# Expert stage of a two-block network: the token gather cut in quarters and spread over the expert pairs, slot gates as one-pass products, expert choice beside group choice

## The chip, the cores and the metric

One core of one Trainium2 chip runs the whole program. The metric is device microseconds (us) of one execution, as the median of several. Durations below come from one profiled execution of the kernel before. Engines: PE is TensorE, DVE is VectorE, ACT is ScalarE, POOL is GpSimd; SP issues most of the transfers.

## The reference, cut to what matters

The program is two blocks over 256 tokens of width 1024. The first block mixes four branches and ends in a wide feed-forward. The second has two layers, each an attention followed by a mixture of experts. The change touches only the mixture of experts, which runs twice:

```python
def moe_ffn(x, router_w, router_b, w_gate, w_up, w_down):      # 256 tokens, 16 experts in 4 groups
    scores = sigmoid(xt @ router_w)
    biased = (scores + router_b).reshape(T, 4, 4)
    group_score = top_k(biased, 2)[0].sum(-1)                   # two best of each group
    best_group = argmax(group_score)
    local = top_k(biased[best_group], 2)[1]                     # two best experts of the best group
    gate = scores[chosen] / sum
    ...                                                         # tokens sorted by expert
    yb = (silu(xi @ w_gate[e]) * (xi @ w_up[e])) @ w_down[e]    # per expert: 1024 -> 256 -> 1024
    y = sum of yb * gate over the token's two experts
```

In front of it stands `layer_norm(ALPHA * x + mixed)`, and another one follows it.

## The kernel before, in words

Activations lie with features on the partitions, as eight blocks of 128 features by 256 tokens. The Tile framework writes out each engine's queue when the program is built. It goes by program order and by its own estimates of what is ready. `behind(ins)` adds an order: what is traced in it is queued after `ins` on that engine. The second block's expert stage (`moe`, L1596) goes like this.

**Routing** (`into_experts` L1404, `route` L1490). Logits come from a small product. On DVE follow sigmoid and bias, then the sum of each group's two best, then `among_first` (L1478), which counts for each entry how many of its four stand before it: once on the group scores (the result is `gb`, the best group) and once on the 16 experts (`sel`). Small products turn `sel` into running counts. `at` is each token's place in an expert's 64 slots, and `places` (L1537) compares it with 1 to 64. The result is `oneh`, one one-hot column for each of 16 x 64 slots. DVE makes `oneh` in four operations of 512 columns (8 experts and 128 tokens each). In between, PE runs products of ones that nobody reads (`warm`, L250): 24 while the routing is computed (`WARM["stats"]`) and 3 before the gather (`WARM["places"]`). The tokens themselves are normalised, transposed and cut in a high and a low part (`tok`, in the trace `s<-half`), four pieces of 256 features. The low parts are DVE's, the first queued behind the group choice, the others behind the last `places`.

**Gather** (L1615). `xg` holds the 1024 slots' tokens, made as one-hot products: a quarter is 256 slots (four experts, two pairs), eight feature blocks, and four one-pass products for each block (two token halves, high and low part). Each feature block has a PSUM bank of the tag `acc` to itself, and ACT and DVE take the blocks in turns to SBUF (`taken`).

**Slot gates** (L1636). 18 products of `oneh` (as plain float32) with the 16 columns of token gates bring each slot's gate to the slot's partition (`gslot`). They run in one batch.

**Expert pairs.** For each pair, `into` (L1664) multiplies the pair's slots with the gate and up weights into the one bank `ps` (32 PE instructions). `hidden` applies silu and the slot gate and transposes through the one bank `tr`. `down` (L1699) multiplies with the down weights into two banks `y`. `across` (L1654) transposes the one-hots, two pairs at a time, into the one tile `oht`. `back` (L1719) adds the pair's result to the four accumulators `acc`. `down` and `back` run one and two pairs late. A ninth pass, the spare one (i = 8), serves one expert with more than 64 tokens. Its weights are fetched by POOL's indirect transfers, since the expert is known only at run time. It stands third in the order (`SPARE = 2`). `late_norm` (L520) normalises the residual in six parts, which are spread over the passes (`LATE`).

**Order of the gather before.** Quarter 0 comes ahead of the first pair's `into`. Quarters 1 and 2, the spare slots' plan and all slot gates come behind it. Quarter 3, the spare slots' gather and two of five `across` come behind the second pair's `into`. The accumulators are allocated only then, since the gather uses their banks.

**Weights** come as pieces of 512 KB: eight for a pair's `into`, four for its `down`, six for the spare pass, 102 in a layer. They land in 21 buffers in turns (13 `raw`, 4 `whi`, 4 `wlo`), so a piece waits until the one 21 before it has been read. SP issues all but the spare ones, in one fixed order.

Of the kernel before, what the change touches and what calls it, by code (L numbers as in the profile page):

```python
# [8 lines left out]
F32 = mybir.dt.float32  # L9
F32R = mybir.dt.float32r  # L10
# [6 lines left out]
D = 1024  # L17
# [184 lines left out]
class Kern:  # L202
# [1275 lines left out]
    def among_first(self, out, val, n, cmp, count):  # L1478

        other = val[:, :, None, :].to_broadcast([128, n, 4, 4])  # L1480
        own = val[:, :, :, None].to_broadcast([128, n, 4, 4])
        self.tt(cmp[:, :, :, 0:4], other, own, OP.is_gt)
        self.tt(cmp[:, :, :, 4:8], other, own, OP.is_equal)
        tri = self.k["tri4"].rearrange("p (a b) -> p a b", a=4)
        self.tt(cmp[:, :, :, 4:8], cmp[:, :, :, 4:8], tri[:, None].to_broadcast([128, n, 4, 4]), OP.mult)
        red = self.A.tile([128, n, 4], F32, name=f"r_red{n}")
        self.nc.vector.tensor_reduce(red, cmp, axis=AX.X, op=OP.add)
        return self.ts(out, red, float(count), OP.is_lt)

    def route(self, sc):  # L1490


        nc, A, X = self.nc, self.A, self.X

        def T(name, *shape):
            return A.tile([128] + list(shape), F32, name=name)
        self.sc, self.bi = sc, X.tile([128, 2, 16], F32, name="r_bi")
        self.ts(sc, sc, 1.0, OP.add)
        nc.vector.reciprocal(sc, sc)
        self.tt(self.bi, sc, self.rb[:, None, :].to_broadcast([128, 2, 16]), OP.add)  # L1500
# [3 lines left out]
        gsf, gtf = (i.rearrange("p t g -> p (t g)") for i in (gs, gt))  # L1504
        self.tt(big, v[:, :, 0:4:2], v[:, :, 1:4:2], OP.max)
# [7 lines left out]
        f4 = lambda t: t.rearrange("p t (g e) -> p (t g) e", g=4)  # L1513
        self.sel = sel = X.tile([128, 2, 16], BF, name="r_sel")
# [71 lines left out]
    def gates(self):  # L1586
# [7 lines left out]
        return sc  # L1594

    def moe(self, layer, x):  # L1596

# [14 lines left out]
            else:  # L1612
                self.ts(out, src, g, OP.mult, o, OP.add)

        def gather(h):  # L1615
            c = slice(h * 256, h * 256 + 256)
            for k in range(8):
                p = self.ps("acc")[:, :256]
                f = slice(k * 128, k * 128 + 128)
                for t in range(2):  # L1620
                    for i in range(2):
                        self.mm(p, xt[i][:, t, f], oh[:, t, c], t == 0 and i == 0, t == 1 and i == 1)
                taken(k, xg[:, k, c], p)

        def gather_spare():
            p = self.ps("acc")
            for k in range(8):
                f = slice(k * 128, k * 128 + 128)
                for t in range(2):
                    for i in range(2):  # L1630
                        self.mm(p[:, k * SLOTS:k * SLOTS + SLOTS], xt[i][:, t, f], ohs[:, t, 0],
                                k == 0 and t == 0 and i == 0, t == 1 and i == 1)
            for k in range(8):
                taken(k, xs_[:, k], p[:, k * SLOTS:k * SLOTS + SLOTS])

        def slot_gates(gates, over):  # L1636

            p = self.ps("tr")
            for i in range(9):
                for t in range(2):  # L1640
                    l = ohf[:, t, i * 128:i * 128 + 128] if i < 8 else ohs[:, t].rearrange("p a s -> p (a s)").bitcast(F32)
                    self.mm(p[:, i * 16:i * 16 + 16], l, gates[:, t], i == 0 and t == 0, t == 1)
            gs = A.tile([128, 9], F32, name="gslot")
            for s in range(2):
                r = slice(64 * s, 64 * s + 64)
                nc.vector.tensor_copy(gs[r, 0:8], p[r, s:s + 8 * 18:18])
            t16 = A.tile([128, 16], F32, name="sp_t2")
            nc.vector.tensor_tensor_reduce(t16, p[:, 128:144], over, 1.0, 0.0, OP.mult, OP.add, accum_out=gs[:, 8:9])
            return gs

        yparts = self.big([128, 2, 2, D])
        yparts = [yparts[:, i] for i in range(2)]

        def across(i):  # L1654

            n = min(2, 9 - i)
            p = self.ps("tr")
            for c in range(2 * n):
                j, t = i + c // 2, c % 2
                o = ohf[:, t, j * 128:j * 128 + 128] if j < 8 else ohs[:, t].rearrange("p a s -> p (a s)").bitcast(F32)  # L1660
                nc.tensor.transpose(p[:, c * 128:c * 128 + 128], o, ident)  # L1661
            self.act(oht[:, i:i + n], p[:, :n * S].rearrange("p (g t) -> p g t", g=n), AF.Copy)

        def into(i):  # L1664

# [53 lines left out]
        def back(i, y, j0, j1, first, last):  # L1719
            for j in range(j0, j1):  # L1720
                f = slice(j * 128, j * 128 + 128)
                for k in range(2):
                    self.mm(acc[j // 2][:, j % 2 * S:j % 2 * S + S], y[:, k, f], oht[:, i],
                            first and k == 0 and j % 2 == 0, last and k == 1)
# [10 lines left out]
        for n, i in enumerate(order):  # L1735
            p = into(i)
            if n == 0:
                gather(1)
                gather(2)
                over, ohs, rows = self.spare(layer)  # L1740
                gs = slot_gates(gates, over)
            elif n == 1:
                wsp = self.spare_weights(rows)
                gather(3)
                gather_spare()
                oht = self.big([128, 9, S])
                across(0)
                across(2)
                acc = [self.ps("acc") for _ in range(4)]
            elif n == 2:  # L1750
                for c in (4, 6, 8):
                    across(c)
            if n in LATE:
                next(norm)
            with self.behind(*self.last_mm):
                if n > 1:
                    back(*ys.pop(0), 0, 8, n == 2, False)
                if prev is not None:
                    ys.append((prev[0], down(*prev)))
            with self.behind(*self.last_mm):  # L1760
                prev = i, hidden(i, p)
        self.raws, self.turn = raws, -1
        back(*ys.pop(0), 0, 8, False, False)
        y = down(*prev)
        self.ln_begin()
# [132 lines left out]
```

## Time and profile before

| | us |
|---|---|
| median of 3 runs | 1334.96 (1331.76 to 1335.94) |
| profiled execution | 1333.13 |
| its span, first to last instruction | 1331.3 |
| PE busy | 1291.8 (97%) |
| DVE busy | 737.2 (55%) |
| ACT busy | 622.5 (47%) |

The expert stage of layer 0 takes roughly 844 to 1012 us of the span and that of layer 1 roughly 1152 to 1313 us. PE's busy share is high all along, but PE matmuls are pipelined and a product at half the clock also counts as busy. So the stage is read by what each batch of products took, by the granted clock of each stretch, and by the chain of work that ended last.

### The profile page before, as it was taken

How to read it: one execution, taken by the hardware profiler on the slowest of the kernel's cores; microseconds unless marked ns; L12 is line 12 of the kernel's file. 1: busy time of each engine (PE TensorE's matmuls, PEld its weight loads, DVE VectorE, ACT ScalarE, POOL GpSimd, SP SyncE). 2: the span in 40 equal slices, each digit the busy share in tenths (PEclk: the TensorE clock that was granted, in tenths of full speed). 3: DMA queues.
4: the chain of work that ended last, by engine and by line, in shares of the span. 5: the costliest groups of instructions: out<-in, count | busy, mean ns of one | idle time of the engine just before them, and what ended most of it. 6: DMA issues, size and time to landing. Idle time of an engine off the chain costs nothing.

```text
span 1331.3 us, 23153 instructions
## 1 busy us (share of the span) xinstructions
PE 1291.8 (97%) x9421; PEld 1073.0 (81%) x9421; DVE 737.2 (55%) x1378; ACT 622.5 (47%) x965; POOL 20.8 (2%) x41
## 2 busy tenths in 40 slices
PE   9999999999999999999999999999998999999996
PEld 7887899999999999999999999573445999664443
DVE  7887665657555556875556463523117676533115
ACT  5756864445544446645454544333115665324112
POOL 0000000000000000000000000010000000010000
PEclk9999999999999999999999999989998999999998
DMA  7441456566486555665555554488995542358992
GB/s 255 129 165 38 133 185 210 180 190 213 160 297 203 184 179 177 187 193 156 169 166 164 163 163 132 163 326 294 407 409 187 158 127 80 127 156 297 380 399 67
DMA packets 90307, 265.16 MB, mean 199 GB/s; under 512 B 26432, under 2 KB 26576, under 8 KB 89936
## 3 DMA queue, kind: packets, MB, share of 16 engines
q1 hardware_dynamic: 86720, 253.07, 57.0%
q0 software_dynamic: 3472, 10.53, 2.3%
q8 instruction: 76, 1.25, 0.4%
q14 instruction: 39, 0.32, 0.1%
HBM read 264.53 MB, written 6.89 MB: 204 GB/s over the span
## 4 chain that ended last, share of the span: by engine, by line
PE 69%; DVE 3%; DMA 2%; ACT 1%; issue 1%; SPq 0%; DVEq 0%; ACTq 0%
PE ps L248 40%; PE acc L248 16%; PE y L248 5%; PE sc L248 3%; PE o L248 2%; PE sc L1252 1%; DMA half<-pP 1%; PE tr L248 1%; DMA raw<-w_sb 1%; ACT whi L234 1%; DVE x L237 1%; DVE wlo L237 1%; PE tr L1694 0%; DMA wlo<-e_gu 0%; PE tr L1661 0%
## 5 line engine op out<-in xcount | busy, mean ns | idle before, releaser
L248 PE MATMUL ps<-s,whi 128*128 128x256 f32 x2656 | 496.1, 286 | 8.2 <-ACT s L234 4.5
L237 DVE TENSOR_TENSOR wlo<-raw,whi 128x1024 fp32r<-128x1024 f32 (+1 forms) x276 | 333.4, 1218 | 260.5 <-ACT whi L234 259.9
L248 PEld LDWEIGHTS ps<-s,whi 128*128 128x128 f32 x2656 | 415.2, 190 | 16.6 <-ACT s L234 5.2
L234 ACT ACTIVATE whi<-raw 128x1024 fp32r<-128x1024 f32 (+1 forms) x276 | 286.6, 1053 | 302.0 <-PE ps L248 221.8
L248 PE MATMUL ps<-s,wlo 128*128 128x256 f32 x1328 | 377.8, 285 | 1.1 <-DVE wlo L237 1.1
L248 PEld LDWEIGHTS ps<-s,wlo 128*128 128x128 f32 x1328 | 251.4, 189 | 3.7 <-DVE wlo L237 2.3
L248 PE MATMUL acc<-hid,whi 128*128 128x256 f32 x512 | 93.2, 282 | 0.0
L248 PE MATMUL ps<-whi,s 128*128 128x256 f32 x512 | 92.3, 282 | 0.0
L248 PE MATMUL ps<-raw,xg 128*64 128x512 f32 x328 | 85.8, 609 | 0.0
L248 PEld LDWEIGHTS ps<-whi,s 128*128 128x128 f32 x512 | 78.3, 188 | 1.5
L248 PEld LDWEIGHTS acc<-hid,whi 128*128 128x128 f32 x512 | 79.2, 189 | 0.2 <-ACT whi L234 0.2
L248 PE MATMUL acc<-hid,wlo 128*128 128x256 f32 x256 | 72.5, 284 | 1.3 <-DVE wlo L237 1.3
L248 PE MATMUL ps<-wlo,s 128*128 128x256 f32 x256 | 71.7, 280 | 0.0
L248 PEld LDWEIGHTS ps<-raw,xg 128*64 128x64 f32 x328 | 25.7, 140 | 44.5 <-issue 41.1
L245 DVE SCALAR_TENSOR_TENSOR eh<-ps,gslot,eh 128x256 f32<-128x256 f32 x16 | 7.7, 484 | 94.0 <-ACT eh L234 94.0
L234 ACT ACTIVATE eh<-ps 128x256 f32<-128x256 f32 x16 | 6.2, 385 | 111.9 <-PE ps L248 111.9
L234 ACT ACTIVATE s<-y 128x512 fp32r<-128x512 f32 x36 | 20.8, 594 | 71.3 <-PE y L248 71.3
L248 PEld LDWEIGHTS acc<-hid,wlo 128*128 128x128 f32 x256 | 47.9, 187 | 1.7 <-DVE wlo L237 1.7
L248 PEld LDWEIGHTS acc<-s,s 128*128 128x128 f32 x288 | 36.0, 190 | 15.7 <-issue 10.7
L248 PEld LDWEIGHTS ps<-wlo,s 128*128 128x128 f32 x256 | 48.2, 188 | 0.0
L248 PE MATMUL acc<-s,whi 128*128 128x256 f32 x256 | 47.8, 286 | 0.3 <-ACT dprobT L234 0.3
L248 PE MATMUL y<-raw,hs 128*64 128x512 f32 x180 | 47.5, 601 | 0.0
(401 smaller groups left out, 1814.3 us busy)
## 6 DMA issues: line engine op xcount, KB each, us to landing
raw<-e_gu SPq DMA_DIRECT2D x82, 512.0 KB, 7.8
raw<-w_dil SPq DMA_DIRECT2D x72, 512.0 KB, 4.5
raw<-w_ff SPq DMA_DIRECT2D x64, 512.0 KB, 4.7
raw<-e_d SPq DMA_DIRECT2D x42, 512.0 KB, 10.1
raw<-w_g SPq DMA_DIRECT2D x32, 512.0 KB, 4.0
raw<-w_a SPq DMA_DIRECT2D x28, 512.0 KB, 4.8
whi<-e_gu SPq DMA_DIRECT2D x27, 512.0 KB, 9.0
raw<-w_sb SPq DMA_DIRECT2D x24, 512.0 KB, 6.6
```

Of the source, the lines that this page charges most:

```text
L234: return self.nc.scalar.activation(out, in_, func, **k)
L237: return self.nc.vector.tensor_tensor(out, a, b, op=op)
L245: return self.nc.vector.scalar_tensor_tensor(out, a, s, b, op0=op0, op1=op1, **k)
L248: self.last_mm = self.nc.tensor.matmul(out, l, r, start=first, stop=last, skip_group_check=True).ins,
L1252: nc.tensor.transpose(pt[:, c * 128:(c + 1) * 128], e[:, order[c]], self.k["ident"])
```

## The change: what it does

Six edits, all in the expert stage.

1. `among_first` becomes a generator. The expert choice starts first, and its operations alternate with those of the group choice; before, it ran behind it. `group_ins`, behind which the first low part is queued, is now whichever choice ended last.
2. `WARM` has 30 and 5 products where it had 24 and 3.
3. `oneh` is made by quarters (two operations of 256 columns each). Quarter 0 precedes the gather, and the others come after quarter 0's gather.
4. The token gates are split in a high and a low part, side by side in 32 columns. The slot gates become one-pass products with `oneh`, four behind each quarter, and DVE adds the two parts (four small reductions for each quarter).
5. One quarter stands ahead of the first `into` and one behind each of the first three. The spare gather comes behind the fourth, and the spare pass is fifth (`SPARE = 4`). A quarter now has two feature blocks to a bank, in `acc` for quarter 0 and in `y`, `y`, `tr`, `y` for the others. The accumulators are allocated right after quarter 0.
6. `across` transposes one pair at a time into one of three tiles, one pass late. `late_norm` starts at the fourth pass (`LATE`).

```diff
-WARM = dict(stats=24, places=3, sums=6, norm=25, start=22)
+WARM = dict(stats=30, places=5, sums=6, norm=25, start=22)
-LATE = (1, 2, 3, 4, 5, 6)
-SPARE = 2
+LATE = (3, 4, 5, 6, 7, 8)
+SPARE = 4
@@ route
+        two = self.among_first(f4(sel), f4(self.bi), 8, T("r_cmp", 8, 4, 8), 2)
         self.tt(big, v[:, :, 0:4:2], v[:, :, 1:4:2], OP.max)
         self.tt(sums, v[:, :, 0:4:2], v[:, :, 1:4:2], OP.add)
+        next(two)
         self.tt(gsf, big[:, :, 0], big[:, :, 1], OP.add)
         self.tt(gtf, sums[:, :, 0], sums[:, :, 1], OP.max)
+        next(two)
         self.tt(gs, gs, gt, OP.max)
-        self.group_ins = self.among_first(gb, gs, 2, T("r_cmp2", 2, 4, 8), 1).ins
-        with self.behind(self.group_ins):
-            self.among_first(f4(sel), f4(self.bi), 8, T("r_cmp", 8, 4, 8), 2)
+        for _ in self.among_first(gb, gs, 2, T("r_cmp2", 2, 4, 8), 1):
+            next(two, None)
+        next(two, None)
...
-        for h in range(2):
-            for t in range(2):
-                self.place_ins = self.places(self.oneh[:, t, 8 * h:8 * h + 8], at[:, t, 8 * h:8 * h + 8])
+        self.one_hots(0)
+    def one_hots(self, c):
+        for t in range(2):
+            self.place_ins = self.places(self.oneh[:, t, 4 * c:4 * c + 4], self.at[:, t, 4 * c:4 * c + 4])
@@ gates
+        parts = A.tile([128, 2, 32], F32R, name="r_gparts")
+        self.nc.vector.tensor_copy(parts[:, :, 0:16], sc)
+        self.tt(parts[:, :, 16:32], sc, parts[:, :, 0:16], OP.subtract)
+        return parts
@@ moe
+        def gather(c, tags):
+            o = slice(c * 256, c * 256 + 256)
+            for k0 in range(0, 8, 2):
+                p = self.ps(tags[k0 // 2]).rearrange("p (b s) -> p b s", b=2)
+                for b in range(2):
+                    f = slice((k0 + b) * 128, (k0 + b) * 128 + 128)
+                    for i in range(2):
+                        for t in range(2):
+                            self.mm(p[:, b], xt[i][:, t, f], oh[:, t, o], b == 0 and i == 0 and t == 0, i == 1 and t == 1)
+                for b in range(2):
+                    taken(k0 + b, xg[:, k0 + b, o], p[:, b])
+            slot_gates([(2 * c, [oh[:, t, 2 * c * 128:2 * c * 128 + 128] for t in range(2)]),
+                        (2 * c + 1, [oh[:, t, 2 * c * 128 + 128:2 * c * 128 + 256] for t in range(2)])])
+        def slot_gates(places):
+            p = self.ps("tr")
+            for n, (i, l) in enumerate(places):
+                for t in range(2):
+                    self.mm(p[:, n * 32:n * 32 + 32], l[t], gates[:, t], n == 0 and t == 0, t == 1)
+            for n, (i, _) in enumerate(places):
...
+                for s in range(2):
+                    r, e = slice(64 * s, 64 * s + 64), n * 32 + 2 * i + s
+                    nc.vector.tensor_reduce(gs[r, i:i + 1], p[r, e:e + 17:16], axis=AX.X, op=OP.add)
...
-        gather(0)
         gates = self.gates()
+        gather(0, ["acc"] * 4)
+        for c in range(1, 4):
+            self.one_hots(c)
         norm = self.late_norm(x, 8 * layer)
+        over, ohs, rows = self.spare(layer)
-        acc, ys = None, []
+        acc, ys = [self.ps("acc") for _ in range(4)], []
         for n, i in enumerate(order):
+            if i == 8:
+                wsp = self.spare_weights(rows)
             p = into(i)
-            if n == 0:
-                gather(1)
-                gather(2)
-                over, ohs, rows = self.spare(layer)
-                gs = slot_gates(gates, over)
-            elif n == 1:
-                wsp = self.spare_weights(rows)
-                gather(3)
-                gather_spare()
-                oht = self.big([128, 9, S])
-                across(0)
-                across(2)
-                acc = [self.ps("acc") for _ in range(4)]
-            elif n == 2:
-                for c in (4, 6, 8):
-                    across(c)
-            if n in LATE:
-                next(norm)
             with self.behind(*self.last_mm):
+                if n < 3:
+                    gather(n + 1, ("y", "y", "tr", "y"))
+                elif n == 3:
+                    gather_spare()
+                if n:
+                    across(order[n - 1])
+                if n in LATE:
+                    next(norm)
                 if n > 1:
                     back(*ys.pop(0), 0, 8, n == 2, False)
                 if prev is not None:
```

## Rows read from the trace of the kernel before

**Rows 1.** The page, part 4: the chain that ended last, shares by engine.

```profile
PE 69%; DVE 3%; DMA 2%; ACT 1%; issue 1%; SPq 0%; DVEq 0%; ACTq 0%
```

**Rows 2.** Windows, layer 0: length, busy of each engine, PE clock, DMA share, GB/s.

```profile
852.70:858.50 5.80, 5.63 (x32) 5.24 (x32) 5.76 (x23) 3.23 (x5) 0.00 (x0) 0.71 0.23 46
...
877.60:889.00 11.40, 11.40 (x45) 4.91 (x44) 1.88 (x7) 0.56 (x1) 0.00 (x0) 0.73 0.84 280
...
960.00:1001.00 41.00, 40.70 (x212) 18.44 (x208) 6.41 (x12) 4.52 (x9) 0.00 (x0) 1.00 1.03 409
```

**Rows 3.** The same view, layer 1.

```profile
1160.80:1167.70 6.90, 6.90 (x34) 6.62 (x34) 6.14 (x24) 3.19 (x5) 0.00 (x0) 0.54 0.01 2
...
1186.50:1196.70 10.20, 10.20 (x45) 3.88 (x44) 1.88 (x7) 0.56 (x1) 0.00 (x0) 0.83 0.39 97
```

**Rows 4.** The chain in order of time, layer 0: start, us, what ran.

```profile
847.34 0.20 DVE r_bi L237
...
849.63 0.60 DVE s L237
...
851.97 2.45 DVE oneh L237 x4
...
858.58 7.02 PE ps L248 x32
865.60 7.87 PE acc L248 x64
873.48 4.20 PE tr L248 x36
877.68 2.11 PE acc L248 x9
...
880.21 8.81 PE ps L248 x32
...
905.14 0.59 ACT half L234
...
905.76 0.60 ACT s L234
...
926.40 4.86 DMA wlo<-e_gu
...
936.66 2.11 PE acc L248 x16
938.77 3.58 PE y L248 x16
942.36 0.37 PE tr L1694 x2
```

**Rows 5.** The same view, layer 1.

```profile
1155.38 0.20 DVE r_bi L237
...
1160.80 6.96 PE acc L248 x32
...
1182.63 3.93 PE tr L248 x36
...
1188.36 8.34 PE ps L248 x32
...
1234.43 7.88 PE ps L248 x31
```

**Rows 6.** PE's timeline, layer 0: start, us, instruction, [idle before <- releaser].

```profile
844.00 5.34 PE L256 MATMUL o<-ones_b 128*128 128x512 bf16 x24
851.39 0.17 PE L248 MATMUL sc<-r_sel,strict_b 128*128 128x16 bf16 x1 [2.04 <-DVE r_sel L237]
```

**Rows 7.** Groups by line, layer 0: count, busy us, mean ns, idle before.

```profile
L234 ACT ACTIVATE xg<-acc,vecs 128x256 f32<-128x256 f32 x16 | 9.1, 566 | 11.6 <-PE acc L248 11.5
```

**Rows 8.** Who waited for whom, 890 to 905 us: us in total, times, longest.

```profile
DVE xspare L242 <- ACT xspare L234: 5.0, 4, 3.4
```

**Rows 9.** DMA issues, 840 to 990 us: count, size, median us to landing.

```profile
raw<-e_gu SPq DMA_DIRECT2D x35, 512.0 KB, 9.4
```

More of the change, by code (lines that the diff above doesn't have):

```diff
@@ L1482, in among_first @@
         self.tt(cmp[:, :, :, 0:4], other, own, OP.is_gt)
+        yield
         self.tt(cmp[:, :, :, 4:8], other, own, OP.is_equal)
+        yield
         tri = self.k["tri4"].rearrange("p (a b) -> p a b", a=4)
         self.tt(cmp[:, :, :, 4:8], cmp[:, :, :, 4:8], tri[:, None].to_broadcast([128, n, 4, 4]), OP.mult)
+        yield
         red = self.A.tile([128, n, 4], F32, name=f"r_red{n}")
         self.nc.vector.tensor_reduce(red, cmp, axis=AX.X, op=OP.add)
-        return self.ts(out, red, float(count), OP.is_lt)
+        yield
+        self.group_ins = self.ts(out, red, float(count), OP.is_lt).ins
     def route(self, sc):
@@ L1593, in gates @@
         self.tt(sc, sc, gw[:, :, None].to_broadcast([128, 2, 16]), OP.mult)
-        return sc
+        if self.dense:
+            return sc
+        parts = A.tile([128, 2, 32], F32R, name="r_gparts")
+        self.nc.vector.tensor_copy(parts[:, :, 0:16], sc)
+        self.tt(parts[:, :, 16:32], sc, parts[:, :, 0:16], OP.subtract)
+        return parts
     def moe(self, layer, x):
@@ L1613, in taken @@
                 self.ts(out, src, g, OP.mult, o, OP.add)
[L1615 to L1619, printed above, removed]
-                for t in range(2):
[L1621 to L1634, printed above, removed]
@@ L1636, in slot_gates @@
-        def slot_gates(gates, over):
-            p = self.ps("tr")
[L1639 to L1662, printed above, removed]
+        def gather(c, tags):
[11 more added lines that the diff above has]
+                        (2 * c + 1, [oh[:, t, 2 * c * 128 + 128:2 * c * 128 + 256] for t in range(2)])])
@@ new lines, in gather_spare @@
+        def gather_spare():
+            for k0 in range(0, 8, 4):
+                p = self.ps("y")
+                for k in range(k0, k0 + 4):
+                    f = slice(k * 128, k * 128 + 128)
+                    c = slice((k - k0) * SLOTS, (k - k0) * SLOTS + SLOTS)
+                    for i in range(2):
+                        for t in range(2):
+                            self.mm(p[:, c], xt[i][:, t, f], ohs[:, t, 0], k == k0 and i == 0 and t == 0, i == 1 and t == 1)
+                for k in range(k0, k0 + 4):
+                    taken(k, xs_[:, k], p[:, (k - k0) * SLOTS:(k - k0 + 1) * SLOTS])
+            slot_gates([(8, [spare(t) for t in range(2)])])
@@ new lines, in moe @@
+        spare = lambda t: ohs[:, t].rearrange("p a s -> p (a s)")
+        gs = A.tile([128, 9], F32, name="gslot")
+        def slot_gates(places):
+            p = self.ps("tr")
+            for n, (i, l) in enumerate(places):
+                for t in range(2):
+                    self.mm(p[:, n * 32:n * 32 + 32], l[t], gates[:, t], n == 0 and t == 0, t == 1)
+            for n, (i, _) in enumerate(places):
+                if i == 8:
+                    t32 = A.tile([128, 2, 16], F32, name="sp_t2")
+                    nc.vector.tensor_tensor_reduce(t32, p[:, n * 32:n * 32 + 32].rearrange("p (k e) -> p k e", k=2),
+                                                   over[:, None, :].to_broadcast([128, 2, 16]), 1.0, 0.0, OP.mult, OP.add,
+                                                   accum_out=gs[:, 8:9])
+                    continue
+                for s in range(2):
+                    r, e = slice(64 * s, 64 * s + 64), n * 32 + 2 * i + s
+                    nc.vector.tensor_reduce(gs[r, i:i + 1], p[r, e:e + 17:16], axis=AX.X, op=OP.add)
@@ L1664, in into, with across @@
+        oht = {}
+        def across(i):
+            p = self.ps("tr")
+            for t in range(2):
+                o = ohf[:, t, i * 128:i * 128 + 128] if i < 8 else spare(t).bitcast(F32)
+                nc.tensor.transpose(p[:, t * 128:t * 128 + 128], o, ident)
+            oht[i] = A.tile([128, S], F32R, name="onehT", bufs=3)
+            self.act(oht[i], p[:, :S], AF.Copy)
         def into(i):
@@ L1727, in moe @@
         self.raws = raws + [("whi", self.W, self.nparts)] * self.nparts + [("wlo", self.W, self.nparts)] * self.nparts
-        gather(0)
         gates = self.gates()
+        gather(0, ["acc"] * 4)
+        for c in range(1, 4):
+            self.one_hots(c)
         norm = self.late_norm(x, 8 * layer)
+        over, ohs, rows = self.spare(layer)
         order = list(range(8))
         order.insert(SPARE, 8)
-        acc, ys = None, []
+        yparts = self.big([128, 2, 2, D])
+        yparts = [yparts[:, i] for i in range(2)]
+        acc, ys = [self.ps("acc") for _ in range(4)], []
         prev = None
         for n, i in enumerate(order):
+            if i == 8:
+                wsp = self.spare_weights(rows)
             p = into(i)
-            if n == 0:
-                gather(1)
-                gather(2)
-                over, ohs, rows = self.spare(layer)
-                gs = slot_gates(gates, over)
-            elif n == 1:
-                wsp = self.spare_weights(rows)
-                gather(3)
-                gather_spare()
-                oht = self.big([128, 9, S])
-                across(0)
-                across(2)
-                acc = [self.ps("acc") for _ in range(4)]
-            elif n == 2:
-                for c in (4, 6, 8):
-                    across(c)
-            if n in LATE:
-                next(norm)
-            with self.behind(*self.last_mm):
+            with self.behind(*self.last_mm):
+                if n < 3:
[6 more added lines that the diff above has]
+                    next(norm)
                 if n > 1:
@@ L1762, in moe @@
         self.raws, self.turn = raws, -1
+        across(7)
         back(*ys.pop(0), 0, 8, False, False)
```

6 lines of the change are left out of this document (3 added, 3 removed).

## The prediction

> **What bounds the kernel now.** I read the page's chain of waits first: TensorE carries 69% of the span and transfers 2% [rows 1], so time can be won only where the expert stage costs PE something, or keeps it from working. The windows come next, for the granted clock. In layer 0 the stretch of quarter 0 ran at a mean of 0.71 of full clock and the second pair's `into` at 0.73; the same two places in layer 1 had 0.54 and 0.83 [rows 2, 3]. Everywhere else in the stage it is 1.00 (2.4 GHz, against 1.2 GHz in the dips). In front of the first dip PE sat idle for 2.04 us [rows 6]; in front of the second it ran the slot gates, short products of 16 columns. Last I read the chain in order of time, for what each batch took: an undisturbed `into` 7.02 us, 64 gather products 7.87 us or 0.123 each, the slot gates 4.20 us for 36 instructions or 0.115 each, and one transfer that PE waited for at 926.40 [rows 4]. So the stage is bound by PE, with five kinds of loss: the wait for the routing, two clock dips, short products in two passes, one late transfer, and a bubble at the spare pass.
>
> **The change part by part.** The sum is made against the profiled execution, 1333.13 us (span 1331.3 and 1.83 around it); it lies 1.83 below the median of the runs, 1334.96.
>
> **A. Routing and quarter 0.** Before, the count products began at 851.39, released by `sel` [rows 6], 3.85 us after `r_bi` ended at 847.54, and 0.60 of it is a low part that DVE slipped into the chain [rows 4]. Alternated, two independent operations overlap their tails. From the chain's steps I count 2.4 us for the 17 operations that must now run before `sel`, and 0.6 for the low part, which can still slip in (queued behind the group choice, it is ready while the last product of `sel` waits for its operand): with the step to PE 3.05, so 0.8 less. The range is 0 (the chain keeps its length) to 1.4 (the low part stays out). The 30 products of ones take 30 x 0.2225 = 6.67 us from 844.00 [rows 6], so until 850.68; the count products are wanted at 850.6. The warm-up now covers the wait, and costs 0.1; if the low part stays out, it costs 0.7, and the range shrinks by as much. Then come 0.28 us of count products and five products of ones, until 852.1. Meanwhile DVE makes `at` and two one-hot operations of 256 columns; four of 512 took 2.45 [rows 4], so about 0.4 each: ready at 852.0. The low parts follow on DVE at 0.60 apiece, the last at 853.8, ahead of the blocks that need them. Quarter 0 is 32 x 0.123 = 3.94, and its slot gates 4 x 0.115 = 0.46. The first `into` starts at 856.5 instead of 858.58: 2.1 less. Layer 1 runs the same chain 308.04 us later (1155.38 for `r_bi`), but its quarter took 6.96 at the low clock and ended at 1167.76 [rows 5]: 3.2 less. This supposes the full clock. If it stays low, quarter 0 takes 6.96 and A becomes a loss of 0.9 in layer 0 and a gain of 0.2 in layer 1. I take 5.3 in all.
>
> **B. Slot gates.** 36 instructions become 18, since a float32 product counts two and the new ones are one-pass, like the gather's. A one-pass product of 32 columns is nowhere in the trace. The old instruction (0.115, 16 columns) and the gather's (0.123, 256 columns) bracket it, whichever way the columns count. 18 x 0.115 = 2.07, of which 0.46 is in A. So 4.20 - 1.61 = 2.6 in layer 0 and 3.93 - 1.61 = 2.3 in layer 1 [rows 4, 5]: 4.9. The parts (two more DVE operations) and 16 reductions in place of two copies lie beside `into` on DVE, which is busy less than a fifth of that stretch [rows 2]; without that cover they cost about 0.5 us a quarter, which F takes in.
>
> **C. The second dip.** With it nine gather products took 2.11 and not 1.11, and `into` 8.81 and not 7.02: 2.8. In layer 1 `into` lost 1.3, and the pair of transposes before it 0.3: 1.6 [rows 4, 5]. No quarter has more than 0.46 us of short products after the change, so I take the dip as gone: 4.4. The lower bound is 0.
>
> **D. The late transfer.** From 926.40 PE had 0.37 of transposes and 7.02 of `into` to do, so until 933.8; it ended at 936.66, 2.9 late. In layer 1 the same `into` took 7.88, 0.9 late [rows 4, 5]. The cause is the order of the buffers: the spare pass owned pieces 17 to 22, so piece 42 could not be fetched until the spare `down` had read piece 21. I count 3.8 as gone; what takes its place is G.
>
> **E. The spare pass.** Behind it PE stood in the chain for an ACT copy of 0.59 and another of 0.60 [rows 4], because four `across` of two pairs were queued on the one bank `tr`. Now one single `across`, a `back` and a full `down` stand there, over 5 us of work: 1.2 less in each layer, 2.4.
>
> **F. New waits on banks (a cost).** Two feature blocks now share a bank. The trace shows what that does: in the spare gather, whose eight blocks shared one, DVE waited for ACT four times, 5.0 us in all [rows 8], while in the quarters each block had its bank and both engines drained side by side. So a bank is free two evacuations of 0.57 [rows 7], about 1.2 us, after its products. PE comes back to the first `y` after two banks, 1.97 us, which is enough. The slot gates follow `tr` after one bank (0.98), which is 0.2 to 0.3 short, and the `across` behind them waits for four reductions, with `down` or the next `into` ready to go ahead. Queued behind a waiting evacuation on DVE are only one-hots and low parts that are wanted microseconds later. I take 0.3 for each of the eight places (three quarters and the spare gather, two layers), 2.4, between 0 and 2.0 each. The Trainium skill speaks against this part: "PSUM — Partial Sum Buffer", Terms, says that two engines must not be on one bank and quadrant at once, reads against reads included. The trace agrees by the row just named. By that rule the two evacuations run one after the other, as taken here; without it the eight places would cost nothing and the sum would come out 2.4 us lower.
>
> **G. New order of the buffers (a cost).** The spare weights become pieces 45 to 50, so pieces 70 and 71 wait until the spare `down` (sixth pass) has read 49 and 50. Piece 70 is the last of the following `into`, wanted 0.37 + 6/8 x 7.02 = 5.6 us later. The transfer that was late before landed 4.86 us after its issue [rows 4], which is in time; the median under load is 9.4 [rows 9], which is 3.8 late. I take 1.0 in each layer, since SP can only be blocked there after most others were issued: 2.0, between 0 and 3.8 each. For the rest, 512 KB at 409 GB/s [rows 2] are 1.28 us, so a pair's twelve pieces take 15.4. The first four pairs now hold PE for up to 17.8 us each (`into` 7.02, gather 4.4, `across` 0.3, `back` 2.11, `down` 3.58, transposes 0.37, rows 4), so the 21 buffers refill there, and SP isn't held up behind 12 us of gather and slot gates in one piece as now. The last pairs (13.4 us each, the same without the gather) eat 2.0 us of that store apiece, 8 in all of the 27 that it holds.
>
> Nothing for the rest: nine ACT copies of 256 columns in place of five wider ones, beside `into`; `late_norm` two passes later, its last part under the last `into` with some 9 us until its result is used (uncovered, about 2.5 us by twice the evacuations of rows 7); the spare transfers on POOL's queue, which holds nothing else then. The accumulators in front free their banks early.
>
> **Sum.** 5.3 + 4.9 + 4.4 + 3.8 + 2.4 = 20.8 gained, 4.4 given back: 16.4. That is 9.5 in layer 0 and 6.9 in layer 1, and everything behind either stage moves up with it. 1333.1 - 16.4 = 1316.7 for an execution like the profiled one, and 1318 against the median.
>
> **Rivals.**
> *The clock stays low.* The batches in front of the dips get denser, which speaks against it; for it, that PE still ends its warm-up within 0.1 us of the count products, and that nothing in the trace shows how much work is enough. A falls from 5.3 to -0.7 and C to 0: 10.4 less gained, 1329.
> *Transfers become the bound.* PE asks for weights 8 to 10 us earlier, and from 960 to 1001 the DMA share is already 1.03 [rows 2]. If SP's fixed order holds pieces back behind 70 and 71, the last four pairs go at 15.4 and not 13.4: up to 8 a layer. Half of that is 1318 + 8 = 1326. Against it: transfers run at 0.01 to 0.23 of their rate during quarter 0 now [rows 2, 3], and the spare pass no longer keeps six buffers empty there.
> *One bank as a chain: slower.* `tr` serves gather, slot gates, `across`, `hidden` and the norm. If PE's queue puts each of them ahead of `down`, every one of eight places waits for an evacuation, four reductions and a copy, about 2.0 us. That is 16 against the 2.4 taken, and such idling may bring back a dip in each layer (1.7 us, as quarter 0 lost in layer 0: 0.29 of 5.80, rows 2). With 2.6 us a place all that is gained is gone: 1337. Against it: before, too, `across` was queued between products of `down`, not ahead.
> *It does not do what it says.* If routing keeps its length, the short products keep their price and the late transfer only moves, little is left: 1332.
>
> **How the numbers follow.** Forecast 62%, with a range of its own of 1310 to 1326 (F and G at nothing, and at half their upper bounds); low clock 16%; transfers 12%; the chain 6%; nothing done 4%. The bounds of the costs and the two middle rivals give a range of 1309 to 1331. A measurement of this kernel can tell about 0.3%, 4 us, so faster is below 1331. Nearly all of the first three cases lies there: 0.86. Without change 0.07: the last case and the edges of the rivals. Slower 0.07: the chain and its neighbours.
>
> **What would show it.** Right: PE not idle between the warm-up and the count products; clock 1.00 in quarter 0 and the second `into`; 18 gate products in batches of four and two; the first `into` near 856.5; the late transfer at the sixth or seventh pass or nowhere. Wrong: waits of PE for `xg`, `gslot` or `oneh` evacuations of over 0.5 us a quarter, transfers ending PE's waits in the last four pairs, or a clock below 1 anywhere in the stage.

## The result, and the profile after

The changed kernel took 1319.03 us (median of 4 runs, 1315.98 to 1321.07), the kernel before on the same chip 1333.86 (4 runs): a ratio of 0.9887, 95% interval 0.9859 to 0.9915. It is faster, by about 15 us; 16.4 was forecast. The profiled execution took 1317.79 us, with a span of 1316.0.

Most readings below are offsets within the expert stage. They count from the copy of `rstd` that opens the routing (843.06 and 1151.1 us in the trace of before, 842.07 and 1141.83 after), because what runs ahead of it moves by some us from one execution to the next. By these offsets, layer 0's stage (to the first product of the next one) shrank from 178.02 to 170.59 us and layer 1's (to the end of the span) from 180.25 to 174.18: 7.4 and 6.1, 13.5 in all. Of the remaining 1.8 us between the two spans, 1.0 lies ahead of the first stage and 0.8 between the stages; neither belongs to the change.

The first view is the page's chain, shares by engine; it answers to [rows 1].

```profile
PE 51%; DVE 2%; ACT 1%; DMA 1%; issue 0%; DVEq 0%; SPq 0%; ACTq 0%
```

Next the chain in order of time at the start of layer 0's stage: start, us, what. In the rows of before the same place went through VectorE's operations ([rows 4], `r_bi` to `oneh`); now it is TensorE from end to end.

```profile
844.90 4.75 PE o L256 x22
849.65 0.17 PE sc L248 x5
849.82 1.13 PE o L256 x5
850.94 3.93 PE acc L248 x32
854.87 1.00 PE ps L248 x2
855.88 0.55 PE tr L248 x4
856.42 5.72 PE ps L248 x25
```

There is no idle time ahead of the count products, quarter 0 takes 3.93, and a batch of four one-pass gates 0.55, which is 0.137 a product. What TensorE itself waited for in layer 0's stage before (engine, tile, releaser: us in total, times, longest):

```profile
PE sc L248 <- DVE r_sel L237: 2.0, 1, 2.0
PE ps L248 <- DMA wlo<-e_gu: 1.8, 1, 1.8
PE ps L248 <- DVE half L237: 1.1, 1, 1.1
PE acc L248 <- ACT s L234: 1.0, 2, 0.7
PE tr L1661 <- ACT s L234: 0.8, 1, 0.8
PE acc L248 <- DVE oneh L237: 0.4, 1, 0.4
```

After, the waits for `r_sel`, for a transfer, at the spare pass (`tr`) and for `oneh` are gone:

```profile
PE acc L248 <- ACT s L234: 1.0, 2, 0.7
PE ps L248 <- DVE half L237: 0.8, 2, 0.5
```

The windows (length, busy of each engine, granted clock, DMA share, GB/s) show quarter 0, then the stretch from there to the spare gather, then the spare gather and the down behind it. They answer to [rows 2].

```profile
850.60:854.90 4.30, 4.30 (x35) 4.06 (x34) 4.29 (x13) 3.81 (x6) 0.00 (x0) 1.00 0.39 95
...
855.70:911.20 55.50, 55.50 (x297) 27.78 (x296) 19.02 (x70) 11.09 (x21) 6.03 (x6) 1.00 0.93 330
...
911.34:924.16 12.82, 12.82 (x69) 9.55 (x70) 2.67 (x8) 2.98 (x7) 0.00 (x0) 0.73 0.83 331
```

Both old dips of the clock are gone. A new one stands where nobody had looked, at the spare gather. It begins at 914.43, 1.0 us before the gather's last product ends, and lasts 6.83. By the profile TensorE was busy for all of the 12.82 us. The chain there:

```profile
904.90 6.44 PE ps L248 x30
911.34 4.12 PE y L248 x32
915.45 0.40 PE tr L248 x2
915.85 1.04 PE acc L248 x4
916.89 0.43 PE tr L1685 x2
917.32 2.56 PE acc L248 x12
919.88 4.28 PE y L248 x16
```

Sixteen `back` products take 3.60 us here, 2.11 at full clock [rows 4]; the down takes 4.28 and not 3.58. Layer 1 has the same dip, shorter: it begins at 1214.80, right behind the gather, and lasts 3.41. Below, a dip "over the spare gather" is one that begins in its last 1.7 us or within 0.6 behind it.

### The profile page after: what moved, and what is told of

Its sections match the earlier page's. It is cut to its first block, busy times and chain, and to the rows that moved or that the text cites. A ratio compares the mean times of both kernels' runs of the same rounds, so it can differ in the third digit from the quotient of the medians.

```text
span 1316.0 us, 23175 instructions
## 1 busy us (share of the span) xinstructions
PE 1285.6 (98%) x9401; PEld 1068.7 (81%) x9401; DVE 741.2 (56%) x1418; ACT 624.4 (47%) x973; POOL 20.8 (2%) x41
## 4 chain that ended last, share of the span: by engine, by line
PE 51%; DVE 2%; ACT 1%; DMA 1%; issue 0%; DVEq 0%; SPq 0%; ACTq 0%
PE ps L248 28%; PE y L248 7%; PE acc L248 7%; PE sc L248 3%; PE o L248 2%; PE o L256 1%; PE tr L248 1%; PE sc L1252 1%; DVE x L237 1%; DMA raw<-w_sb 1%; PE tr L1685 0%; PE tr L1719 0%; ACT whi L234 0%; PE acc L1422 0%; DVE wlo L237 0%
## 5 line engine op out<-in xcount | busy, mean ns | idle before, releaser
L248 PE MATMUL ps<-raw,xg 128*64 128x512 f32 x324 | 80.7, 597 | 0.0
L237 DVE TENSOR_TENSOR s<-y,s 128x512 fp32r<-128x512 f32 x36 | 24.3, 685 | 55.6 <-ACT s L234 55.6
L248 PE MATMUL acc<-onehT,s 128*128 128x256 f32 x288 | 45.5, 307 | 1.7 <-ACT s L234 1.7
```

The source lines that it names most:

```text
L237: return self.nc.vector.tensor_tensor(out, a, b, op=op)
L248: self.last_mm = self.nc.tensor.matmul(out, l, r, start=first, stop=last, skip_group_check=True).ins,
```

## The experiments

Each ratio is to the kernel before on the same chip, with its 95% interval; the ends of the intervals lie 2 to 4 us from their middles, so differences of 1 to 3 us are read from the traces. The theory at the start: the gain comes from the routing, the gates, the lost dips and the late transfer, as the prediction had it, less what the new dip at the spare gather costs. The rival: the dips cost little where they stood, and the gain has other sources.

**The change once more**, unchanged.

> The changed kernel as it is, as the measure for the runs beside it: 13 to 17 us below the kernel before, and a stretch at half clock behind the spare gather of either layer, as in the profile taken of it before (6.83 us in layer 0, 3.41 us in layer 1).

1317.3 us (6 runs), ratio 0.9890 (0.9864 to 0.9916). The lengths of the two stages repeat to 0.05 us, and a dip stands over the spare gather of both layers again (it begins at 918.42 and 1218.79).

**Spare gather 128 columns wide.** The same 32 products write both one-hot copies of the spare; half of what they write is not read.

```
-  c = slice((k - k0) * SLOTS, (k - k0) * SLOTS + SLOTS)
+  c = slice((k - k0) * 128, (k - k0) * 128 + 128)
-  self.mm(p[:, c], xt[i][:, t, f], ohs[:, t, 0], ...)
+  self.mm(p[:, c], xt[i][:, t, f], spare(t), ...)
```

> The changed kernel, but the spare gather's 32 products write 128 columns each (both copies of the one-hots) and not 64; the second half is never read. Theory: the dip that the changed kernel shows behind this gather comes from its short products. Then the granted clock stays at 1.00 there, the accumulating products behind it take 1.9 us again and not 3.6 (layer 0) and 3.3 (layer 1), and the time falls by 3.1 + 1.5 = 4.6 us, to some 14 to 20 us below the kernel before. Rival: the dip comes from something else in that pass (its transposes, PE's waits), or products of 128 columns last longer: then the dip stays, or the gather's 32 products take more than 3.7 us, and the time is the changed kernel's or up to 2 us above it.

1315.52 us, ratio 0.9879 (0.9855 to 0.9902). The chain over the same place:

```profile
903.92 6.44 PE ps L248 x30
910.36 3.72 PE y L248 x32
914.08 0.18 PE tr L248 x2
914.26 0.57 PE acc L248 x4
914.83 0.22 PE tr L1685 x2
915.05 1.43 PE acc L248 x12
916.48 3.58 PE y L248 x16
```

No dip. Twice the columns took 0.03 us longer than the 64 do at full clock (3.69), and from the spare gather to the end of the down it is 9.70 us and not 12.82: 3.1 less. In layer 1 it is 1.5 less, but the last down of that layer, with its last weights not yet there, took 4.95 and not the changed kernel's 3.93. A second study of the same kernel:

> The same kernel as in the run with a spare gather of 128 columns, once more, on the chip that takes the three kernels beside it. Theory: it has no dip of the clock in either layer's expert stage, whatever the execution, and the first weight product to the last down takes 134 to 136 us in each layer; time 1314 to 1317. Rival: that the dip was missing there was chance; then the granted clock is at half somewhere between the spare gather and the down behind it again, and the time is that of the changed kernel, 1317 to 1320.

1315.25 us, ratio 0.9858 (0.9843 to 0.9873), and no dip in either layer's stage. The window over the spare gather and the down:

```profile
912.70:922.40 9.70, 9.70 (x70) 7.05 (x68) 2.75 (x8) 2.87 (x7) 0.00 (x0) 1.00 1.02 408
```

Over all kernels with one-pass gates, a dip stood over the spare gather of 64 columns in 11 of 16 stages (8 profiles, two layers each) and over that of 128 columns in none of 8. So these short products bring the dip at this place; whether it comes varies between executions. With the old float32 gates the same gather of 64 columns had no dip in any of 4 stages: there the dip stood at the gates, 12 to 15 us earlier.

**Old warm-up in the changed kernel.**

```
-  WARM = dict(stats=30, places=5, ...)
+  WARM = dict(stats=24, places=3, ...)
```

> The changed kernel with 24 and 3 products of ones, as before, and not 30 and 5. Theory: PE then waits some 1.2 us for the expert choice, and the dip at quarter 0 comes back: quarter 0 takes 5.7 to 7.0 us and not 3.93, 2 to 3 us more in each layer, so 4 to 6 us above the changed kernel. Rival: the shorter routing is enough by itself; quarter 0 stays at 3.93, the clock at 1.00, and the time is the changed kernel's within 1 us.

1316.51 us, ratio 0.9887 (0.9862 to 0.9911). The theory fell: with 1.20 us of idle time ahead of the count products the clock stayed at full in quarter 0, in both layers.

```profile
854.00:858.40 4.40, 4.12 (x34) 3.92 (x33) 4.40 (x14) 3.91 (x7) 0.00 (x0) 1.00 0.43 130
```

**New warm-up in the kernel before.**

```
-  WARM = dict(stats=24, places=3, ...)
+  WARM = dict(stats=30, places=5, ...)
```

> The kernel before with 30 and 5 products of ones as its only change. Theory: the dip at quarter 0 follows from PE's 2.04 us of idling, which shrink to 0.7; the clock stays at 1.00 there, quarter 0 loses 1.7 us in layer 0 and some 3 in layer 1, and the time falls by 4 to 5 us against the kernel before. The second dip, behind the slot gates, stays. Rival: the 0.7 us that are left, or the products around them, still bring the dip; then the time is the kernel before's within 1 us.

1331.94 us, ratio 0.9996 (0.9980 to 1.0012). The dip at quarter 0 went, as expected; the time did not follow. The window of quarter 0, then the chain:

```profile
853.10:858.90 5.80, 4.77 (x35) 4.19 (x36) 5.80 (x23) 3.37 (x5) 0.00 (x0) 1.00 0.20 58
```

```profile
852.37 2.45 DVE oneh L237 x4
854.82 1.80 DVE s L237 x3
856.63 0.47 DVE xg L242
857.10 0.04 issue
857.14 1.70 PE acc L248 x12
```

At full clock TensorE is idle for 1.0 of 5.8 us, and VectorE is busy for all of it: four one-hots of 512 columns, then three low parts that the products need. The first `into` started 15.30 after the copy of `rstd`, against 15.46 and 16.59 in the two layers before. The clock was worth 0.16 and 1.29 us there; VectorE's queue set the time. In layer 1 of this execution a piece of weights also came 2.33 us late, with a dip of 3.41 behind it (1238.63), where the kernel before lost 0.9; so the total of this execution is not quarter 0's alone.

**All one-hots ahead of quarter 0.**

```
-  self.one_hots(0)
-  for c in range(1, 4): self.one_hots(c)
+  for h in range(2):
+      for t in range(2):
+          self.place_ins = self.places(self.oneh[:, t, 8*h:8*h+8], at[:, t, 8*h:8*h+8])
```

> The changed kernel, with the one-hot copies of all four quarters made ahead of quarter 0 (four operations of 512 columns, as in the kernel before), instead of those of quarter 0 alone (two of 256). Theory: the routing's gain of step A is for the larger part VectorE's: quarter 0 was held by the one-hots in front of it, not by the clock. Then quarter 0 starts 1.2 to 1.7 us later in each layer (four one-hots took 2.45 us, two of 256 about 0.8), the first pair's weight products too, and the run is 2.4 to 3.4 us longer than the changed kernel, about 1322 (1320 to 1324). Rival: the gain of A is that of the shorter choice of experts and of the clock; the one-hots are made while the products of ones run. Then the first pair's weight products start within 0.5 us of the changed kernel's and the time stays at 1319.

1319.62 us, ratio 0.9912 (0.9894 to 0.9930). The first `into` starts 13.52 after the copy in both layers, not 12.74: 0.78 later, where the theory had 1.2 to 1.7 and the rival under 0.5. The direction is the theory's, the size lies between the two. The total can't tell: its ratio is 0.0022 to 0.0025 above the change's two, which the intervals are too wide for, and dips come and go beside it (the profiled execution had one short dip over layer 0's spare gather and none in layer 1).

**Expert choice behind the group's again.**

```
-  for _ in self.among_first(gb, gs, 2, ...):
-      next(two, None)
+  for _ in self.among_first(gb, gs, 2, ...):
+      pass
+  with self.behind(self.group_ins): ...
```

> The changed kernel with the choice of experts run behind the choice of groups again and not beside it (step A's first term undone alone). Theory: r_sel ends 0.84 us later, and so do quarter 0 and the first weight products, in both layers; with nothing else the run is 1.7 us longer, 1319 to 1321. Rival: the longer wait of TensorE between the products of ones and the count products brings back a dip of the clock at quarter 0, as the kernel before had one there; then 1 to 2.7 us more in a layer, and the granted clock shows it at the start of the stage.

1319.23 us, ratio 0.9883 (0.9865 to 0.9901). `r_sel` ends 0.85 later, and the first `into` starts at 13.59 and 13.57: 0.84 later in each layer. No dip at quarter 0, so the rival is out. The total can't show these 1.7 us: they are less than its interval, and in the profiled execution layer 0's spare gather had no dip.

**Spare pass third again.**

```
-  SPARE = 4
+  SPARE = 2
+  if n == 1: gather_spare()
   if n < 3: gather(n + 1, ("y", "y", "tr", "y"))
-  elif n == 3: gather_spare()
```

> The changed kernel with the spare pass third again, as before (its gather behind the second pair's weight products, ahead of quarter 2), so that it owns pieces 17 to 22 again. Theory (D): the late transfer was due to that order of the buffers. Then TensorE waits again for a weight transfer in the pass behind the spare's down, by up to 2.9 us in layer 0 and 0.9 in layer 1, and the run is 2 to 4 us longer, 1321 to 1323. Rival: the transfer was late because SP stood behind 12 us of gather and slot gates in one piece; with the gather spread the demand is even and the place of the spare pass makes no difference: no transfer ends a wait of TensorE of over 0.5 us there, 1319.

1317.95 us, ratio 0.9891 (0.9871 to 0.9911). TensorE's waits in layer 0's stage, with no transfer among them:

```profile
PE ps L248 <- DVE half L237: 1.1, 1, 1.1
PE acc L248 <- ACT s L234: 1.0, 2, 0.7
```

Layer 1's stage has no such wait either. The theory fell: the order of the buffers alone does not make the transfer late.

**Gather in front, spare pass fifth.**

```
-  if n < 3: gather(n + 1, ...)
+  if n == 0: gather(1, ...); gather(2, ...)
-  elif n == 3: gather_spare()
+  elif n == 1: gather(3, ...); gather_spare()
```

> The changed kernel with quarters 1 and 2 both behind the first pair's weight products and quarter 3 behind the second's (the spare gather stays behind the fourth's): the places that the kernel before gave them, in the new banks and with one-pass gates. Theory: the spread by itself moves no work of TensorE; its use is that weights are asked for evenly. If the spare pass's place is what made the transfer late, no wait of TensorE for weights appears and the time stays within 1.5 us of the changed kernel's, 1317.5 to 1320.5. Rival: the spread is what took the late transfer away: TensorE waits 2 us or more in each layer for weights in the third to fifth pass, 1322 to 1325.

1320.77 us, ratio 0.9917 (0.9896 to 0.9937). The edit moved more than was meant: the spare gather went along and stands right behind quarter 3, in the second pass. So the whole gather is where the kernel before had it, and the spare pass alone stays fifth. No wait for a transfer here in layer 0 either; the dip over the spare gather is there in both layers (889.53 and 1189.90, 6.83 each). In layer 1 weights came late at another place: the last pair's `into` took 7.74 and not 7.02. In layer 0, then, the late transfer needs both, the gather in two pieces in front and the spare pass third, and each half of the change alone removes it, in one trace each. The next two kernels have both, and the wait (1.6 and 2.1 us in layer 0). A dip that gave the transfer time is not the reason, since the first of them has the same dip (889.49, 6.83).

**One-pass gates in the kernel before.**

```
-  self.mm(p[:, i*16:i*16+16], ohf[:, t, ...], gates[:, t], ...)
+  self.mm(p[:, i*32:i*32+32], oh[:, t, ...], gates[:, t], ...)
```

(`gates` as two parts of 16 columns, and reductions over the pairs; one batch at the old place.)

> The kernel before with one edit: the gates of places as one-pass products of 32 columns (18 in place of 36 instructions, still in one batch at the old place). Theory (B and C): the batch falls from 4.20 and 3.93 to 2.1 to 2.6 us in each layer (18 x 0.115 to 0.137), and the clock's dip in the second pair's weight products was due to 36 short products in a row, so it goes or shrinks: 3.2 us for the products and up to 4.4 for the dip, 1326 to 1331 where the kernel before has 1334. Rival: the dip has another cause (for instance the idle time ahead, or the gather's own products) and stays; then only the batch gets shorter, and 1330 to 1332 results, with a clock near 0.73 in that stretch as before.

1324.1 us, ratio 0.9945 (0.9928 to 0.9963): 7.8 us below the kernel before on the same chip (1331.94), where the theory had 3 to 8 and the rival 2 to 4. Chain of layer 0: the gates, the rest of the gather, and the second `into`, which stands at 8.81 in [rows 4].

```profile
873.39 1.92 PE tr L248 x18
875.31 2.97 PE acc L248 x24
878.28 0.22 PE tr L1703 x2
878.50 7.02 PE ps L248 x32
885.52 5.14 PE acc L248 x40
```

The dip behind the gates is gone in both layers; it stood there in all 4 stages with the old gates. In layer 0 one came over the spare gather instead (889.49, 6.83), and the one at quarter 0 stayed (851.94, 3.41). In layer 1 there is none: its last down starts at 146.58 after the copy of `rstd`, against 152.40 before. That is 5.8 us less, 1.3 of it at quarter 0 and 0.8 at the transfer that was late before (that `into` took 7.07 and not 7.88); 3.7 come from 18 instructions in place of 36 and the clock behind them. The gates' number, width and float32 form changed together, and no run tells these apart.

**Both kinds of short products gone, nothing else.** The same, with the spare gather 128 columns wide.

> The kernel before with two edits and none of the new order: the one-pass gates in one batch, and the spare gather 128 columns wide. Theory: the short products were what pulled the clock down in the stage's first passes; with both kinds of them gone the dip that remained in layer 0 with the gates alone (889.49, over the spare gather and the down behind it) goes too, 3 to 4 us there, and the time is 1319 to 1322, which is three quarters of the whole gain without any of the spreading. Rival: a dip follows the idle places of this order (the routing's wait, the spare pass's 0.75 us), and comes back in some other place; then it stays at 1323 to 1326.

1321.1 us, ratio 0.9911 (0.9898 to 0.9925), as the theory had it: 8.9 thousandths off, where the change took off 11.0 and 11.3 in its two studies, and 14.2 with the wide spare gather on this same chip. The only dip left in the two stages is at quarter 0 of layer 0 (851.27, 3.41), behind 2.04 us of idle time. What the old order still costs stands in TensorE's waits in layer 0's stage:

```profile
PE ps L248 <- DMA wlo<-e_gu: 2.1, 1, 2.1
PE sc L248 <- DVE r_sel L237: 2.0, 1, 2.0
...
PE tr L1672 <- ACT s L234: 0.8, 1, 0.8
PE acc L248 <- DVE oneh L237: 0.4, 1, 0.4
```

**Last down ahead of the back before it**, with the wide spare gather.

```
+  y = down(*prev)
   back(*ys.pop(0), 0, 8, False, False)
-  y = down(*prev)
```

> The kernel with the spare gather of 128 columns, and the last pair's down put ahead of the back of the pair before it, so that this back lies over the evacuation of the last down, which TensorE waited 0.6 to 0.7 us for. Theory: each layer ends 0.6 us sooner, 1313.5 to 1315. Rival: the last weights decide; the last two pieces of layer 1 landed only 1.9 us before the last down ended, so its down only waits longer, layer 1 gains nothing or loses up to 2 us, and the time is 1315 to 1317.

1316.5 us, ratio 0.9868 (0.9852 to 0.9883): no gain over the kernel without it. Layer 0's stage is the same to 0.01 us; layer 1's is 0.45 shorter. Why layer 0 gained nothing the runs do not settle. The chain at layer 1's end shows why there is not more there:

```profile
1284.63 2.10 PE y L248 x8
1286.72 0.91 PE acc L248 x6
1287.63 2.38 PE y L248 x8
1290.01 2.00 PE acc L248 x15
```

TensorE's queue interleaves the two anyway, and the last two pieces, issued at 1282.50 and 1283.28 when the down before had read their buffers, landed at 1286.00 and 1288.03, inside this down.

## Why the prediction was right

The time was 1 us off, and the case forecast is the one that happened, but part of that is luck. The two stages gained 13.5 us and not 16.4 (7.4 and 6.1, where the forecast's terms add up to 9.4 and 7.0 and it says 9.5 and 6.9); 1.8 us that lie outside the stages make up for most of the difference. Inside, the dip that C overlooked cost 4.6, and the costs F and G, which hardly came, gave 4.2 back. The steps, in us for both layers together, as offsets in the traces give them:

```
step                              predicted  measured
A routing and quarter 0               5.3       5.5
B slot gates                          4.9       4.2
C second dip gone                     4.4      -0.2
D late transfer                       3.8       3.7
E bubble at the spare pass            2.4       1.5
F waits on banks                     -2.4       0
G order of the buffers               -2.0      -0.2
rest (by difference)                  0        -1.0
sum                                  16.4      13.5
```

**A** came out in size, with the wrong reason in layer 1. The first `into` starts 2.72 and 3.86 earlier; less 0.55 a layer for quarter 0's gates, which now stand behind its first two products, that is 2.2 and 3.3 for the forecast 2.1 and 3.2. But the prediction gave the clock about 3 us of layer 1's quarter 0 (6.96 against 3.94). The warm-up alone gave the clock back and left the time as it was; what counts is the shorter choice (0.84 a layer) and the one-hots in pieces (0.78), one behind the other on VectorE, and the 0.16 and 1.29 that the dip did cost. Undone one at a time, the first two make 1.62 of the 2.56 us a layer between the kernel with the new warm-up alone and the change (15.30 and 12.74). On VectorE's queue the one-hots ahead of the low parts shrank from 2.45 to 0.76, which with the 0.84 is 2.53; undone alone they cost less than that 1.69, as the chain there then no longer runs through VectorE. The warm-up itself was not needed for the clock.

**B**: the value was taken from the old instruction (0.115) and bracketed by 0.123; the new one took 0.137 in batches of four. In one batch of 18 it took 1.92, 0.107 each, so it is the small batch that costs more, and the bracket missed on both sides.

**C is the step that failed.** It said that the dip goes because no quarter has more than 0.46 us of short products. That is true of the gates, and the run with one-pass gates alone confirms that they caused the old dip. It overlooked the spare gather: 32 products of 64 columns, which now stand in one piece behind a pair's `into`. A dip came there and took 3.1 and 1.5 us, 4.6 against the 4.4 that were won. The low clock was among the rivals, but for a different place and cause; "a clock below 1 anywhere in the stage" stood among the prediction's signs of being wrong, and it came. The Trainium skill, "TensorE: Matmul & The Clock Gate", section "HAM oscillation — how this bites in real kernels", puts such dips down to idle gaps of TensorE, waits for DMA in its example; for the dip at the spare gather this trace doesn't agree, since TensorE was busy for 12.82 of 12.82 us while the clock fell, and for 55.50 of 55.50 us ahead of them.

Idle time did go with the dips at quarter 0. Behind the 2.04 us of the old routing a dip came in 4 of 6 stages (three kernels), behind 0.7 to 1.2 us in none of 6 (three others). Of the five waits for weights of 0.9 to 2.3 us in the old order, the longest alone had a dip with it.

**D** had the size right (2.86 and 0.86 in the two layers) and half of the cause: with the gather spread the transfer is in time even in the old order of the buffers. Among kernels with the old order the size varies, though: the wait was 0.9 to 2.1 us in layer 0 of four traces.

**E** took ACT's two copies as fully exposed; TensorE's wait there was 0.8 in each layer.

**F** was priced from VectorE's waits, which did come: 6.2 us in 12 waits for the `xg` of ACT in layer 0, where [rows 8] had 4 for `xspare`. (Of the 5.0 us in [rows 8], 3.4 stand ahead of the first copy, while the gather itself still ran.)

```profile
DVE xg L242 <- ACT xg L234: 6.2, 12, 0.8
```

But TensorE was idle for 0.34 us in all between the end of the routing and the last down of layer 0. The queue had other products ready, so these waits of VectorE cost TensorE no idle time; the 0.3 a place were a guess between bounds, and the lower one came.

**G**: the pass that it feared for, behind the spare down, lost nothing. Layer 1's last down took 3.9 and not 3.7, the only place where a late piece shows, and more where the rest is shorter (4.95 with the wide spare gather).

The rest is what is left by difference. One loss in it is seen: quarter 0's gates now cut the first pair's `into`, whose two parts took 1.00 and 7.01 us where an uncut one takes 7.02, so 1.0 in each layer. That is more than the rest comes to, and no run takes apart what gave the other 1.0 back. What the result leaves open is the choice of the place at which a dip falls: with 64 columns it came in 11 of 16 stages, and no run here tells which ones are spared.

The best version measured is the change with the spare gather at 128 columns: 0.9879 and 0.9858 in its two studies, the change 0.9887 and 0.9890. Their intervals overlap; its stages are 3.6 us shorter in layer 0 and 1.1 in layer 1, alike in both of its traces.

## What to carry to other kernels

Where the granted clock is under 1 while TensorE is busy, look for a batch of short products in front of that place, and not for idle time alone. Making such batches fewer or wider took 8.9 thousandths off the time here; together with all the rest of the change it was 14.2. When such a batch is gone, list the batches that remain and check each for the same fault, because the dip can come at the next one. A product at half clock costs only what the engine that feeds it doesn't already take: here 0.16 us of a dip of 3.41.

## What the runs showed that was not expected

Thirty-two products took 3.69 us at 64 columns where no dip fell on them (the chain of the kernel with the expert choice behind the group's, layer 0, below), 3.72 at 128, and 3.93 at 256.

```profile
914.86 3.69 PE y L248 x32
```

Up to 256 columns, width was nearly free here, and the wider form of the spare gather kept the clock. What cost more was a small batch between other work: four gates of 32 columns took 0.55, which is 0.137 each and more than the gather's 0.123 with 256, while 18 of the same in a row took 1.92, which is 0.107 each.
